# A fourth chunk by seven products in the gate/up groups of a two-layer decoder trunk, with merged combinations and h transposes in one bank

## The chip, the cores and the metric

The kernel runs on one core of a Trainium2 chip. TensorE (PE) multiplies matrices into PSUM, which has eight banks of 512 float32 columns; VectorE (DVE) and ScalarE (ACT) work element by element on SBUF and PSUM; SyncE (SP) issues most of the transfers. Each engine takes its instructions in the order in which they stand in its own list, and waits on semaphores for what other engines have to deliver. The metric is the device time of one execution, in microseconds (us).

## The reference

For 256 tokens of width 2048 two layers are computed: a token mixer (trailing means in layer 0, differential attention with eight heads in layer 1), then a dense SwiGLU block, each with an RMS norm in front and a residual addition behind.

```python
def swiglu(h, wg, wu, wd):
    return (jax.nn.silu(h @ wg) * (h @ wu)) @ wd
...
        h = h + mix
        h = h + swiglu(rmsnorm(h, norm_ffn[i]), w_gate[i], w_up[i], w_down[i])
    return rmsnorm(h, final_norm)
```

`w_gate` and `w_up` are 2048 x 5632, `w_down` is 5632 x 2048, all float32. The change is about `h @ wg` and `h @ wu`.

## The kernel before

**Precision.** Every large product is made from float32 numbers split in two: a rounded half `hi` (ScalarE, a cast) and the remainder `lo` (VectorE, a subtraction). One block product is three matmuls, hi by hi, hi by lo and lo by hi, each 128 x 128 by 128 x 512.

**Groups and chunks.** The 5632 columns of gate and up are done in 11 groups of 512 + 512 columns. A group runs over eight chunks of 256 weight rows (called p0 to p7 here), one 1 MB load each (`load`, three buffers `raw`). A chunk is a 2 x 2 by 2 x 2 block product: two halves of the tokens, two halves of the rows, gate and up. A *plain* chunk makes the eight block products, 24 matmuls. A chunk *by sevens* (`SEVEN`: p2, p4 and p6; in group 0 of layer 0 p6 alone) uses Winograd's scheme of seven products, 21 matmuls. For it VectorE makes four sums of weight blocks (`sums`, L121, L123, L124), ScalarE rounds them (`thi`, L130) and VectorE makes their remainder (`tlo`, L131); the weight halves `whi` (L115) and `wlo` (L116) then need only three of the four blocks. There is one buffer each for `tsum`, `thi` and `tlo`, and three for each of `whi` and `wlo`. The token sums are made once, where the operand is transposed (`pair`).

**Banks.** The products of all chunks of a group add up in the eight banks, named M1, M6, M7, P5, P3, P4, M2 and X (0 to 7); plain chunks use M2, P3, P4 and X. At the end of a group `combined` makes gate and up from them: two copies on ScalarE and eight additions on VectorE, of 512 columns each (L201 to L211). Then come silu (L463, ScalarE), the product with up (L464, VectorE), and for the two new pairs of h tiles four 128 x 128 transposes each (L250, PE), written to a bank from `aux`, which takes banks 0 to 3 in turn; ScalarE and VectorE read them into the operand of the down product (L254, L255, or L263 to L268 where the down product takes the pair by sevens).

**Order.** Groups come in chunks of 4, 4 and 3; after each such set there are two groups of the down product (`w_down`), with residual additions at their end (L487). The program is written in this order, and a scheduler of the framework, which has its own estimates, fixes the order in each engine's list. Loads, halves and sums of the next group's first chunks stand there ahead of or between the combinations of the group before.

## Time and profile before

| | |
|---|---|
| median of three runs | 1845.46 us (1845.2 to 1845.46) |
| profiled execution, its own time | 1846.21 us |
| its span from first to last instruction | 1844.4 us |
| granted TensorE clock, mean | 0.997 |
| PE / DVE / ACT busy | 1829.2 / 1604.2 / 1038.0 us |
| transfers | 356.80 MB, 193 GB/s |

A row of the profile that groups instructions has the line, the engine, the operation, out<-in by the program's names, the shapes and the count; behind the bar the busy time in us and the mean of one in ns; behind the second bar the engine's idle time before them and what ended it. A row of the timeline has the start and the duration in us; in brackets stands the idle time before it and who ended it. A row of a table of stretches has, for each engine, busy us and the count, then the granted clock, the share of the transfer engines and GB/s.

### The profile page before, as it was taken

The numbers are of one execution on the slowest core, as the hardware profiler recorded it, in microseconds if no ns is written. First come the engines' busy times: TensorE is split into PE (matmuls) and PEld (weight loads), VectorE is DVE, ScalarE is ACT, GpSimd is POOL, SyncE is SP. The second block draws the span as 40 slices with busy tenths as digits, with TensorE's granted clock in tenths as the row PEclk, the third lists the DMA queues.
The fourth block names the chain that finished last, engine by engine and source line by source line (L and its number), as shares of the span: only waits on it lengthen the run. The fifth ranks groups of instructions, "written<-read, shape, count | busy, mean of one in ns | idle before, by whom it ended". The sixth has DMA issues, their size and how long they took to land.

```text
span 1844.4 us, 20901 instructions
## 1 busy us (share of the span) xinstructions
PE 1829.2 (99%) x8210; PEld 1495.6 (81%) x8210; DVE 1604.2 (87%) x1662; ACT 1038.0 (56%) x1006; POOL 0.7 (0%) x6
## 2 busy tenths in 40 slices
PE   9999999999999999999999999999999999999998
PEld 6788888888888888888888888788888888888886
DVE  6889998898989899988888678998989899998986
ACT  6555555555554556665566655555555555545553
POOL 0000000000000000000000000000000000000000
PEclk9999999999999999999999999999999999999999
DMA  7555555655555555555454454555555555565552
GB/s 273 183 201 187 193 210 194 210 196 194 203 198 204 202 186 183 208 180 171 173 177 164 160 188 176 205 203 187 204 205 204 188 201 183 206 227 204 206 186 111
DMA packets 50642, 356.80 MB, mean 193 GB/s; under 512 B 6000, under 2 KB 6128, under 8 KB 8048
## 3 DMA queue, kind: packets, MB, share of 16 engines
q1 hardware_dynamic: 49824, 353.85, 54.4%
q10 hardware_dynamic: 720, 1.62, 0.2%
q8 instruction: 64, 1.05, 0.2%
q14 instruction: 34, 0.28, 0.0%
HBM read 353.36 MB, written 2.10 MB: 193 GB/s over the span
## 4 chain that ended last, share of the span: by engine, by line
PE 95%; DVE 2%; ACT 1%; issue 1%; DMA 1%; SPq 0%; DVEq 0%; ACTq 0%
PE b L180 90%; PE b L250 2%; PE b L342 1%; DVE wlo L116 1%; PE b L554 1%; PE b L345 1%; PE b L584 0%; DMA w<-pool_w 0%; DMA raw<-w_gu 0%; DVE tlo L131 0%; ACT whi L115 0%; DVE tsum L121 0%; PE b L600 0%; PE b L598 0%; PE b L599 0%
## 5 line engine op out<-in xcount | busy, mean ns | idle before, releaser
L115 ACT CAST whi<-raw 128x1536 fp32r<-128x1536 f32 (+1 forms) x330 | 585.2, 1774 | 585.4 <-PE b L180 499.6
L180 PE MATMUL b<-whi,xp 128*128 128x512 f32 x2824 | 908.8, 392 | 1.2 <-DVE c L203 1.0
L116 DVE TENSOR_TENSOR wlo<-raw,whi 128x1536 fp32r<-128x1536 f32 (+1 forms) x330 | 697.3, 2113 | 193.1 <-ACT whi L115 192.9
L180 PEld LDWEIGHTS b<-whi,xp 128*128 128x128 f32 x2824 | 528.3, 188 | 110.1 <-DVE c L203 1.5
L180 PE MATMUL b<-wlo,xp 128*128 128x512 f32 x1412 | 551.8, 391 | 1.6 <-DVE wlo L116 1.6
L180 PE MATMUL b<-whi,h 128*128 128x512 f32 x1108 | 354.5, 390 | 0.0
L180 PEld LDWEIGHTS b<-wlo,xp 128*128 128x128 f32 x1412 | 265.3, 188 | 55.5 <-DVE wlo L116 1.9
L131 DVE TENSOR_TENSOR tlo<-tsum,thi 128x2048 fp32r<-128x2048 f32 x108 | 246.7, 2285 | 3.9 <-ACT thi L130 3.9
L180 PEld LDWEIGHTS b<-whi,h 128*128 128x128 f32 x1108 | 207.5, 188 | 43.1
L180 PE MATMUL b<-wlo,h 128*128 128x512 f32 x554 | 215.8, 389 | 0.0
L130 ACT CAST thi<-tsum 128x2048 fp32r<-128x2048 f32 x108 | 206.3, 1910 | 13.7 <-DVE tsum L124 13.6
L180 PE MATMUL b<-thi,xp 128*128 128x512 f32 x608 | 211.8, 390 | 0.0
L121 DVE TENSOR_TENSOR tsum<-raw 128x1024 f32<-128x1024 f32 x108 | 131.8, 1220 | 2.3 <-DMA raw<-w_v 0.6
L180 PEld LDWEIGHTS b<-thi,xp 128*128 128x128 f32 x608 | 113.9, 188 | 24.0 <-ACT thi L130 0.9
L180 PEld LDWEIGHTS b<-wlo,h 128*128 128x128 f32 x554 | 104.0, 188 | 21.3
L180 PE MATMUL b<-tlo,xp 128*128 128x512 f32 x304 | 119.5, 393 | 0.0
L180 PE MATMUL b<-thi,h 128*128 128x512 f32 x240 | 83.7, 389 | 0.0
L124 DVE TENSOR_TENSOR tsum<-tsum,raw 128x512 f32<-128x512 f32 x108 | 74.3, 688 | 2.3
L123 DVE TENSOR_TENSOR tsum<-tsum,raw 128x512 f32<-128x512 f32 x108 | 73.9, 684 | 0.6
L180 PE MATMUL b<-whi,oT 128*128 128x512 f32 x236 | 74.4, 392 | 0.0
L180 PEld LDWEIGHTS b<-tlo,xp 128*128 128x128 f32 x304 | 57.0, 188 | 16.1 <-DVE tlo L131 4.4
L180 PEld LDWEIGHTS b<-thi,h 128*128 128x128 f32 x240 | 45.1, 188 | 9.2
(147 smaller groups left out, 1192.5 us busy)
## 6 DMA issues: line engine op xcount, KB each, us to landing
raw<-w_gu SPq DMA_DIRECT2D x176, 1024.0 KB, 4.9
raw<-w_down SPq DMA_DIRECT2D x88, 1024.0 KB, 4.8
raw<-w_qk SPq DMA_DIRECT2D x32, 1024.0 KB, 4.9
raw<-w_v SPq DMA_DIRECT2D x16, 1024.0 KB, 4.8
raw<-w_o SPq DMA_DIRECT2D x16, 1024.0 KB, 4.8
raw<-pool_w SPq DMA_DIRECT2D x2, 1024.0 KB, 13.8
x_tok<-x_n SPq DMA_DIRECT2D x2, 768.0 KB, 9.0
w<-pool_w SPq DMA_DIRECT2D x2, 512.0 KB, 6.6
```

Source lines behind the costliest of these rows:

```text
L115: nc.scalar.copy(hi[:, lo_block:], raw[:, lo_block:])
L116: nc.vector.tensor_tensor(lo[:, lo_block:], raw[:, lo_block:], f32(hi[:, lo_block:]), ALU.subtract)
L121: nc.vector.tensor_tensor(t[:, T1:T3 + 1], raw[:, B11:B22 + 1], raw[:, B12:B12 + 1].broadcast_to([P, 2, 512]), ALU.add)
L123: nc.vector.tensor_tensor(t[:, T2], t[:, T1], raw[:, B22], ALU.add)
L124: nc.vector.tensor_tensor(t[:, T4], t[:, T2], raw[:, B21], ALU.add)
L130: nc.scalar.copy(hi, t)
L131: nc.vector.tensor_tensor(lo, t, f32(hi), ALU.subtract)
L180: nc.tensor.matmul(ps[b], x, y[:, block], start=first, stop=(left[b] == 0))
L250: nc.tensor.transpose(ps[:, i, 1 - t if seven else t], src(i, t), ident)
L342: nc.tensor.matmul(yp[g][t], a[:, rows], w[:, at], start=(at == 0), stop=(at == 3))
L345: nc.tensor.matmul(yp[g][t], u, v[:, at], start=(at == 0 and j == 0), stop=(at == 3 and j == 2))
L554: nc.tensor.matmul(sc[:, :nk], qk[:, 0, c, qb * P:(qb + 1) * P], qk[:, 1, c, :nk], start=True, stop=True)
```

## The change

`SEVEN` becomes (0, 2, 4, 6): p0 is done by sevens too, in groups 1 to 10 of both layers (group 0 of layer 0 keeps p6 alone, group 0 of layer 1 keeps p2, p4 and p6). In a chunk by sevens the three products of raw weight blocks come first (P3 only late in a group's first chunk), and the products of sums follow. P3 and P4 become one tile of two banks, b45, and `combined` works on both at once: two subtractions become one of 1024 columns (L211), two additions one (L212). The transposes of h go to bank X (7) instead of the banks 0 to 3. To make room in SBUF for p0's larger operand, constants live shorter (`ones`, `dist_sb`, whose load moves to the attention's start), `part` uses other small tiles, and four of the heads' outputs use the operand's buffers.

```diff
-SEVEN = (2, 4, 6)
+SEVEN = (0, 2, 4, 6)
...
+    def two_banks():
+        both = psum.tile([P, 2, 512], F32, name="b45", tag="b45")
+        return [both[:, i] for i in range(2)], both
...
             if seven:
-                plan.append([(M1, [(A11, 0, B11)]), (M2, [(A12, 0, B21)]), (M6, [(S2, 1, T2)]), (M7, [(S3, 1, T3)]),
-                             (P5, [(S1, 1, T1)]), (P3, [(S4, 0, B22)]), (P4, [(A22, 1, T4)])])
+                raw = [(M1, [(A11, 0, B11)]), (M2, [(A12, 0, B21)]), (P3, [(S4, 0, B22)])]
+                summed = [(P5, [(S1, 1, T1)]), (M7, [(S3, 1, T3)]), (M6, [(S2, 1, T2)]), (P4, [(A22, 1, T4)])]
+                late = 3 if plan else 2
+                plan.append(raw[:late] + summed[:3] + raw[late:] + summed[3:])
...
-            first = b not in ps
-            if first:
+            first = b not in opened
+            opened.add(b)
+            if first and b in (P3, P4) and b not in ps:
+                (ps[P3], ps[P4]), ps["both"] = two_banks()
+            elif first and b not in ps:
                 ps[b] = bank(b)
...
-        m1, u2, u3, p5 = (pool.tile([P, 512], F32, name=f"c{i}") for i in ("11", "12", "21", "22"))
+        c = pool.tile([P, 4, 512], F32, name="c")
+        m1, u2, u3, p5 = (c[:, i] for i in range(4))
...
-        nc.vector.tensor_tensor(u2, p5, u2, ALU.subtract)
-        nc.vector.tensor_tensor(p5, p5, u3, ALU.subtract)
-        nc.vector.tensor_tensor(u2, ps[P3], u2, ALU.add)
-        nc.vector.tensor_tensor(u3, ps[P4], u3, ALU.add)
+        nc.vector.tensor_tensor(c[:, 1:4:2], c[:, 3:4].broadcast_to([P, 2, 512]), c[:, 1:3], ALU.subtract)
+        nc.vector.tensor_tensor(c[:, 1:3], ps["both"], c[:, 1:3], ALU.add)
...
-    def pair(dst, src, gains, seven):
+    def pair(dst, src, gains, seven, at=None):
 
-        ps = aux((P, 2, 2, P))
+        ps = aux((P, 2, 2, P)) if at is None else bank(at, (P, 2, 2, P))
...
-                    by_seven = SEVEN[-1:] if g == 0 and layer == 0 else SEVEN
+                    by_seven = SEVEN if g else SEVEN[1:] if layer else SEVEN[-1:]
...
-                        pair(ht, lambda k, t: cs[t][1][:, (2 * i + k) * P:(2 * i + k + 1) * P], None, at in SEVEN_DOWN)
+                        pair(ht, lambda k, t: cs[t][1][:, (2 * i + k) * P:(2 * i + k + 1) * P], None, at in SEVEN_DOWN, X)
...
+        dist_sb = hq.tile([P, 2 * P], F32, name="dist_sb")
+        nc.sync.dma_start(out=dist_sb, in_=dist)
```

In the changed kernel the sums are L120, L122 and L123, whi L114, wlo L115, thi L129, tlo L130, the matmuls L184, the combinations L206 to L214, silu L469, the product with up L470, the h transposes L253, their reads L257, L258 and L266 to L271, the residual additions L493. There are 20 groups that begin with p0 by sevens: 16 follow a gate/up group, four a down group. The lists differ at the transitions, in three ways.

**Place one, VectorE between the third and the fourth group of layer 0** (c is the third group's gate and up; with a prime for the next group, wlo_1407 and tsum_1398 belong to p0', wlo_1441 to p1', raw_1468 and wlo_1475 to p2'). Before:

```order
L116 TENSOR_TENSOR wlo_1441<-raw_1438,whi_1440 128x2048
L207 TENSOR_TENSOR c22_1367<-c22_1367,c21_1366 128x512
L208 TENSOR_TENSOR c12_1365<-b4_1114,c12_1365 128x512
L209 TENSOR_TENSOR c21_1366<-b5_1121,c21_1366 128x512
L211 TENSOR_TENSOR c22_1367<-b7_1128,c22_1367 128x512
L464 SCALAR_TENSOR_TENSOR c12_1365<-c12_1365,r_tok_496,c11_1364 128x512
L464 SCALAR_TENSOR_TENSOR c22_1367<-c22_1367,r_tok_496,c21_1366 128x512
L123 TENSOR_TENSOR tsum_1470<-tsum_1470,raw_1468 128x512
L116 TENSOR_TENSOR wlo_1475<-raw_1468,whi_1474 128x1536
```

Of the changed kernel:

```order
L209 TENSOR_TENSOR c_1361<-b2_1120,c_1361 128x512
L123 TENSOR_TENSOR tsum_1398<-tsum_1398,raw_1396 128x512
L211 TENSOR_TENSOR c_1361<-c_1361 128x2x512
L115 TENSOR_TENSOR wlo_1475<-raw_1468,whi_1474 128x1536
L212 TENSOR_TENSOR c_1361<-b45_1128,c_1361 128x1024
L214 TENSOR_TENSOR c_1361<-b7_1159,c_1361 128x512
L470 SCALAR_TENSOR_TENSOR c_1361<-c_1361,r_tok_496 128x512 x2
L130 TENSOR_TENSOR tlo_1407<-tsum_1398,thi_1406 128x2048
```

The remainder of p2' (wlo_1475) has moved from behind the combinations to ahead of the last two, and a new tlo, of p0', stands behind them. Eight of the 16 transitions between gate/up groups have this order.

**Place two, PE at the same transition** (xp_76, xp_78 and xp_79 are the operands of p0', p2' and p3' in the changed kernel, xp_83 that of p0' before; the transposes are those on ident). Before:

```order
L180 MATMUL b5_1424<-whi_1406,xp_83 128x512
L250 MATMUL b2_1383<-ident_75,c12_1365 128x128
L250 MATMUL b3_1397<-ident_75,c12_1365 128x128
L180 MATMUL b5_1424<-whi_1406,xp_83 128x512
L180 MATMUL b5_1424<-wlo_1407,xp_83 128x512
L250 MATMUL b2_1383<-ident_75,c22_1367 128x128
```

Of the changed kernel, from the 15th matmul behind the group's last one on:

```order
L184 MATMUL b6_1414<-wlo_1475,xp_78 128x512
L184 MATMUL b6_1414<-whi_1474,xp_78 128x512
L184 MATMUL b45_1430<-whi_1402,xp_76 128x512
L184 MATMUL b45_1430<-wlo_1403,xp_76 128x512
L184 MATMUL b45_1430<-whi_1402,xp_76 128x512
L184 MATMUL b45_1430<-thi_1406,xp_76 128x512
L253 MATMUL b7_1375<-ident_74,c_1361 128x128 x4
L184 MATMUL b6_1414<-whi_1505,xp_79 128x512
L253 MATMUL b7_1389<-ident_74,c_1361 128x128 x4
L184 MATMUL b3_1418<-tlo_1407,xp_76 128x512
```

Between a group's last matmul and the first that reads tlo of p0' there stand 23 matmuls now (11 on thi of p0' or behind it, up to the transposes), and all eight transposes, of which the second four wait until bank 7 has been read.

**Place three: ScalarE between the sixth and the seventh group of layer 0** (c_2811 is the sixth group; whi_2924 belongs to p2', thi_2856 to p0', whi_2955 to p3', e and h are reads of the h transposes; before, whi_2939 belongs to p2' and whi_2974 to p3'), **and VectorE from a down group to gate/up.** ScalarE before:

```order
L463 ACTIVATE c11_2829<-c11_2829,r_tok_496 128x512
L115 CAST whi_2939<-raw_2933 128x1536
L463 ACTIVATE c21_2831<-c21_2831,r_tok_496 128x512
L263 ACTIVATE e_2853<-b0_2848 128x256
L263 ACTIVATE e_2853<-b0_2848 128x2x128
L254 CAST h_2861<-b1_2862 128x2x256
L115 CAST whi_2974<-raw_2972 128x2048
```

Of the changed kernel:

```order
L469 ACTIVATE c_2811<-c_2811,r_tok_496 128x512
L114 CAST whi_2924<-raw_2918 128x1536
L129 CAST thi_2856<-tsum_2848 128x2048
L469 ACTIVATE c_2811<-c_2811,r_tok_496 128x512
L114 CAST whi_2955<-raw_2953 128x2048
L266 ACTIVATE e_2830<-b7_2825 128x256
```

A thi has come in behind whi of p2' and ahead of the second silu. On VectorE there the order is L212, L214, the first L470, tlo of p0', the second L470, wlo of p1'; seven transitions are like this. VectorE from a down group to gate/up before (wlo_2306 belongs to p1', tsum_2335 to p2'):

```order
L487 TENSOR_TENSOR x_tok_82<-c22_2254,x_tok_82 128x512
L116 TENSOR_TENSOR wlo_2306<-raw_2303,whi_2305 128x2048
L123 TENSOR_TENSOR tsum_2335<-tsum_2335,raw_2333 128x512
L116 TENSOR_TENSOR wlo_2340<-raw_2333,whi_2339 128x1536
L124 TENSOR_TENSOR tsum_2335<-tsum_2335,raw_2333 128x512
```

Of the changed kernel (wlo_2292 belongs to p1', tsum_2250 and tlo_2259 to p0'):

```order
L212 TENSOR_TENSOR c_2235<-b45_1986,c_2235 128x1024
L214 TENSOR_TENSOR c_2235<-b7_1999,c_2235 128x512
L493 TENSOR_TENSOR x_tok_75<-c_2235,x_tok_75 128x512 x3
L123 TENSOR_TENSOR tsum_2250<-tsum_2250,raw_2248 128x512
L115 TENSOR_TENSOR wlo_2292<-raw_2289,whi_2291 128x2048
L130 TENSOR_TENSOR tlo_2259<-tsum_2250,thi_2258 128x2048
```

The last sum of p0' now stands behind the residual additions, and its tlo behind wlo of p1'; ahead of the first matmul on thi of p0' PE has 12 matmuls.

More of the change, by code (lines that the diff above doesn't have):

```diff
@@ L84, in trunk_kernel @@
     gain_sb = const.tile([P, 6, NK], F32, name="gain_sb")
-    dist_sb = const.tile([P, 2 * P], F32, name="dist_sb")
     ident = const.tile([P, P], F32, name="ident")
-    ones = const.tile([P, P], F32, name="ones")
-    nc.vector.memset(ones, 1.0)
-    make_identity(nc, ident)
     x_tok = resid.tile([P, 2, D], F32, name="x_tok")
@@ L152, in group @@
                 left[b] = left.get(b, 0) + 3 * len(parts)
-        ps = {}
+        ps, opened = {}, set()
         def prepared(seven, src):
@@ L280, in trunk_kernel @@
     with tc.tile_pool(name="start", bufs=1, reuse_waits="tile") as st:
+        ones = st.tile([P, P], F32, name="ones")
+        nc.vector.memset(ones, 1.0)
         warm = tmp.tile([P, 8], F32, name="warm", bufs=1)
+        make_identity(nc, ident)
         nc.scalar.activation(warm[:, 0:1], ones[:, 0:1], AF.Sqrt)
@@ L334, in product @@
             if some[0] == 0:
-                yp[g] = [bank(4 + 2 * (g % 2) + t) for t in range(2)]
+                yp[g] = [bank(6 + t) for t in range(2)] if g % 2 else two_banks()[0]
                 if g >= PLAIN:
@@ L413, in trunk_kernel @@
     turn["of"] = 4
-    nc.sync.dma_start(out=dist_sb, in_=dist)
     def finish(cs, ys, final_sb, ss):
         for t in range(2):
-            part = tmp.tile([P, 64], F32, name="part", bufs=2)
+            part = tmp.tile([P, 8], F32, name="warm", bufs=1) if t == 0 else \
+                tmp.tile([P, 2, 4], F32, name="ss").rearrange("p a b -> p (a b)")
             nc.vector.tensor_reduce(part[:, 0:1], ss[:, t, 0:2], AX.X, ALU.add)
@@ L515, in trunk_kernel @@
         nc.vector.tensor_scalar(qs_col, r_col, QK_SCALE, None, ALU.mult)
+        ones = hq.tile([P, P], F32, name="ones")
+        nc.vector.memset(ones, 1.0)
         nc.vector.tensor_tensor(lp, lam_sb[:, 0:2], lam_sb[:, 2:4], ALU.mult)
@@ L608, in trunk_kernel @@
                     nc.scalar.activation(on[:, t, :], op[:, t, :], AF.Copy, scale=ro[:, t:t + 1])
-                oT[h] = op_.tile(pair_shape(h in SEVEN_O), F32R, name=f"oT{h}")
+                if h < 4:
+                    oT[h] = op_.tile(pair_shape(h in SEVEN_O), F32R, name=f"oT{h}")
+                else:
+                    oT[h] = resid.tile(pair_shape(h in SEVEN_O), F32R, name="xp", tag=f"xp{h}")
                 pair(oT[h], lambda i, t: on[:, t, i * P:(i + 1) * P], [gs[:, i:i + 1] for i in range(2)], h in SEVEN_O)
```

## The prediction

> **What bounds the kernel now.** I read the page first: busy shares, then the chain that ended last.
>
> ```profile
> PE 1829.2 (99%) x8210; PEld 1495.6 (81%) x8210; DVE 1604.2 (87%) x1662; ACT 1038.0 (56%) x1006; POOL 0.7 (0%) x6
> ...
> PE 95%; DVE 2%; ACT 1%; issue 1%; DMA 1%; SPq 0%; DVEq 0%; ACTq 0%
> PE b L180 90%; PE b L250 2%; PE b L342 1%; DVE wlo L116 1%; PE b L554 1%; PE b L345 1%; PE b L584 0%; DMA w<-pool_w 0%; DMA raw<-w_gu 0%; DVE tlo L131 0%; ACT whi L115 0%; DVE tsum L121 0%; PE b L600 0%; PE b L598 0%; PE b L599 0%
> ```
>
> TensorE sets the end: 90% of the chain are the matmuls of L180. VectorE's 87% is a mean, so I looked at single stages: two gate/up groups (eight chunks and eight h transposes each) and one down group without transposes.
>
> ```profile
> core 0: us, PE busy (x) PEld busy (x) DVE busy (x) ACT busy (x) POOL busy (x), PEclk, DMA share, GB/s
> 340.00:382.43 42.43, 42.43 (x193) 35.09 (x192) 37.66 (x33) 23.06 (x18) 0.00 (x0) 1.00 0.57 198
> 425.15:467.88 42.73, 42.73 (x193) 35.01 (x192) 38.87 (x37) 24.18 (x20) 0.00 (x0) 1.00 0.56 197
> 510.62:552.10 41.48, 41.48 (x185) 34.35 (x184) 37.56 (x34) 20.64 (x14) 0.00 (x0) 1.00 0.57 203
> ```
>
> The down group issues 3 x 21 + 5 x 24 = 183 matmuls in 41.48 us (two of the 185 counted overlap the edges): 0.2267 us each. The same 183 with eight transposes take 42.73, so the transposes cost 1.25. In that gate/up group VectorE has only 42.73 - 38.87 = 3.86 us left.
>
> **The change part by part.** Removed: 20 chunks (chunk 0 of groups 1 to 10, both layers) go from 24 matmuls to 21: 60 x 0.2267 = 13.6 us of TensorE. Added on VectorE and ScalarE, by these rows:
>
> ```profile
> L116 DVE TENSOR_TENSOR wlo<-raw,whi 128x2048 fp32r<-128x2048 f32 x222 | 508.1, 2289 | 178.8 <-ACT whi L115 178.7
> L131 DVE TENSOR_TENSOR tlo<-tsum,thi 128x2048 fp32r<-128x2048 f32 x108 | 246.7, 2285 | 3.9 <-ACT thi L130 3.9
> L130 ACT CAST thi<-tsum 128x2048 fp32r<-128x2048 f32 x108 | 206.3, 1910 | 13.7 <-DVE tsum L124 13.6
> L116 DVE TENSOR_TENSOR wlo<-raw,whi 128x1536 fp32r<-128x1536 f32 x108 | 189.2, 1752 | 14.3 <-ACT whi L115 14.2
> L115 ACT CAST whi<-raw 128x1536 fp32r<-128x1536 f32 x108 | 160.4, 1485 | 210.0 <-PE b L180 157.1 <-DVE c L209 33.7 <-issue 16.8
> L487 DVE TENSOR_TENSOR x_tok<-c,x_tok 128x512 f32<-128x512 f32 x44 | 28.3, 683 | 0.0
> L254 ACT CAST h<-b 128x512 fp32r<-128x512 f32 x28 | 15.9, 592 | 12.5 <-PE b L250 12.5
> ```
>
> What VectorE holds up is less than a duration, since the next one starts before the last has ended. The timeline of a transition between groups shows the steps, and what ScalarE waits for there:
>
> ```profile
> 425.75 1.22 DVE L121 TENSOR_TENSOR tsum<-raw 128x1024 f32<-128x1024 f32 x1
> 426.88 0.68 DVE L204 TENSOR_TENSOR c<-b,c 128x512 f32<-128x512 f32 x1
> 427.48 0.68 DVE L203 TENSOR_TENSOR c<-b,c 128x512 f32<-128x512 f32 x1
> ...
> 428.68 2.28 DVE L116 TENSOR_TENSOR wlo<-raw,whi 128x2048 fp32r<-128x2048 f32 x1
> 430.88 0.68 DVE L207 TENSOR_TENSOR c<-c,c 128x512 f32<-128x512 f32 x1
> ...
> 433.28 1.40 DVE L464 SCALAR_TENSOR_TENSOR c<-c,r_tok,c 128x512 f32<-128x512 f32 x2
> 434.60 0.68 DVE L123 TENSOR_TENSOR tsum<-tsum,raw 128x512 f32<-128x512 f32 x1
> 435.20 1.75 DVE L116 TENSOR_TENSOR wlo<-raw,whi 128x1536 fp32r<-128x1536 f32 x1
> 436.87 0.41 DVE L264 TENSOR_TENSOR e<-e 128x256 f32<-128x256 f32 x1
> ```
> ```profile
> 431.24 1.48 ACT L115 CAST whi<-raw 128x1536 fp32r<-128x1536 f32 x1 [2.32 <-PE b L180]
> 432.80 0.72 ACT L463 ACTIVATE c<-c,r_tok 128x512 f32<-128x512 f32 x1
> 435.63 0.66 ACT L263 ACTIVATE e<-b 128x256 f32<-128x256 f32 x2 [2.11 <-PE b L250]
> ```
>
> From start to start: 2.20 for 2048 columns, 1.67 for 1536, 1.13 for 1024, 0.60 for 512, 0.66 for L464. One more seven costs VectorE 1.13 + 2 x 0.60 + 2.20 - (2.20 - 1.67) = 4.0 us. No row shows the merged combinations (L211, L212); they lie between L121's 1.13, the same size, and two single steps, 1.20. I take 1.13, which saves 4 x 0.60 - 2 x 1.13 = 0.14 a group. So VectorE needs 38.87 + 3.86 = 42.73 in such a group, TensorE 42.73 - 0.68 = 42.05: **VectorE has no spare time left**, and whatever it does late TensorE feels.
>
> Late it will be at the transitions. Write p0 to p7 for a group's chunks, p0' for the next group's, and T for the moment at which TensorE could issue the matmul behind the group's last. The weight halves have three buffers, so whi of p2' takes p7's and cannot start before T + 0.2: a matmul lasts 0.39 by the row below, 0.16 beyond the next issue, and the reader's start is rounded up.
>
> ```profile
> L180 PE MATMUL b<-whi,xp 128*128 128x512 f32 x2824 | 908.8, 392 | 1.2 <-DVE c L203 1.0
> ```
>
> The row at 431.24 is that wait: 2.32 us, and harmless, because p0' and p1' were plain chunks, prepared, with 48 matmuls (10.9 us) for TensorE. Now p0' is a seven. Its raw products are 9 matmuls; the other 12 need thi and tlo.
>
> *Transitions of the first kind* (8 of 16; front part, places one and two). ScalarE: whi of p2' ends at T + 1.7. VectorE has wlo of p2' ahead of L212: 1.7 + 1.67 = 3.4; L212 to 4.5, L214 to 5.1, two L470 to 6.4, tlo of p0' to 8.7. ScalarE goes on with silu (0.72) and thi of p0' (1.91), to T + 4.25; from there TensorE has 11 matmuls to 6.75 and four h transposes (half of 1.25) to 7.4. The second four want the same bank, which ScalarE reads behind whi of p3'; that cast waits for P3 of p0' (T + 6.7) and ends at 8.65, the two reads (0.66) at 9.3. The transposes end at T + 10.0, and only then come the matmuls on tlo. Done by then: 23 x 0.2267 + 1.25 = 6.5 us. **Lost: 3.5 us.** Where both h pairs are plain (4 of the 8) the bank is free after a cast (0.59, from 8.65) and a subtraction (0.68), transposes end at 10.5, and 28 matmuls and the eight transposes are done, 7.6: lost 2.9.
>
> *Second kind* (7; place three, ScalarE). thi of p0' stands behind whi of p2': T + 1.7 + 1.9 = 3.6. Then tlo to 5.9, the second L470 to 6.5, wlo of p1' to 8.8. Ahead of wlo of p1' TensorE has 24 matmuls and the transposes, 6.7: lost 2.1. The next sums (of p2') end on VectorE about T + 15.3, their cast behind whi of p4' at 17.4, while 57 matmuls and 1.25 are 14.2: 3.2 lost in all.
>
> *From a down group to gate/up* (4; place three, VectorE). L212 can end at T + 0.8, L214 at 1.4, three residual adds (L487's step 0.60) at 3.2, the last sum at 3.8, thi at 5.8. TensorE has 12 matmuls, 2.7: lost 3.1. Nothing is lost there now.
>
> The first transition of layer 0 has p0' fully prepared: 0. From gate/up to down, p0' stays plain: 0. **Sum:** 4 x 3.5 + 4 x 2.9 + 7 x 3.2 + 4 x 3.1 = 60.4, less 13.6: +46.8. At the low end only the first waits count (2.2 from tlo's T + 8.7 against 6.5; 2.1; 3.1): 8 x 2.2 + 7 x 2.1 + 12.4 - 13.6 = +31. At the high end VectorE, without spare time, adds 1 us to each of the 16: +63.
>
> At no cost I take: raw products first (they only cover more); the merged sums outside gate/up, where VectorE is not late; the loads, equal in number, with dist's moved among them on SP's queue; and p0's operand laid out for sevens, 1.2 us more of VectorE twice, which if not covered is +2.4.
>
> **The clock.** Stalls of 3 us may also lower it. Two stretches of the profile's clock grid, each with what followed:
>
> ```profile
> 4.80:8.21 3.41, 1.80 (x12) 1.20 (x11) 1.36 (x3) 0.72 (x2) 0.00 (x0) 1.00 0.96 340
> 8.21:11.62 3.41, 3.41 (x7) 1.39 (x6) 0.48 (x1) 0.67 (x1) 0.00 (x0) 0.50 1.03 429
> 52.58:56.00 3.42, 1.77 (x10) 1.31 (x9) 2.73 (x2) 3.11 (x5) 0.00 (x0) 1.00 0.24 34
> 56.00:59.41 3.41, 3.13 (x16) 2.36 (x15) 3.41 (x5) 1.32 (x3) 0.00 (x0) 1.00 0.68 279
> ```
>
> TensorE was busy 1.80 of 3.41 us, and the next 3.41 ran at 0.50; busy 1.77, and they ran at 1.00. The margin lies near there, and the single 3.1 us gap behind a down group would pass it; a stretch at half clock costs 3.41 / 2 = 1.7 us. The Trainium skill, "TensorE: Matmul & The Clock Gate", section "What's actually happening", says that the clock is halved after at least one idle window of about 3.4 us. By that rule none of my gaps halves it, and the sum stays; the first of the rows above does not bear it out, since that window was half busy.
>
> **The rivals.** (1) *TensorE stays the bound*: what is late hides behind products that the new order finds. 1846.2 - 13.6, less 0.75 for the median: 1832. For it: 99% busy now, and waits of VectorE and ScalarE hidden everywhere. Against it: rows of fixed order and duration behind one fixed event, T. (2) *VectorE becomes the bound and keeps pace*: 16 groups with a seven among their h at 42.73 as now, the four others at 41.75 instead of 42.43: -2.7, 1843, no change. Against it: it must never wait, and it waits 1.5 us for whi of p2' at half the transitions. (3) *The half clock*: the four gaps behind down groups and the seven of the second kind, each up to 1.7: +19, 1911. It decides from the point at which a gap fills about half a window. (4) *Loads late as well*: chunk p5's buffer comes free only with p2's last sum, and landing takes 4.9:
>
> ```profile
> raw<-w_gu SPq DMA_DIRECT2D x176, 1024.0 KB, 4.9
> ```
>
> With that VectorE is a further 2 us late in 16 groups: +79 in all, 1924.
>
> **How the numbers follow.** The sum is made on the profiled execution, 1846.2, which is 0.75 above the median: 1846.2 + 46.8 - 0.75 = 1892. Chances: my forecast 0.66, (1) 0.09, (2) 0.06, (3) 0.12, (4) 0.07. The forecast's own range is 1872 to 1910. To 1864 at the low end for transitions that lose less, to 1926 at the high end for (3) and (4). A measurement of this kernel tells about 0.2% (3.7 us) from no change: faster 0.09, same 0.06, slower 0.85.
>
> **What would show it.** In the changed profile: 60 fewer matmuls; PE's share under 97%; idle time of PE and PEld before L184 and L253 on tlo, thi and wlo, 2 to 4 us at a transition; gate/up groups of 44 to 45.5 us followed by gate/up, under 42.3 where down follows; ScalarE's whi on 1536 columns still released by PE at T. Wrong would be: transitions without idle TensorE (1), VectorE without any idle time in a group (2), a clock under 0.99 (3), or whi waiting for raw<-w_gu (4).

## The result and the profile after

The changed kernel takes 1933.85 us (median of 4 runs, 1933.13 to 1934.39) where the kernel before took 1845.33 beside it: a ratio of 1.048, 95% interval 1.0461 to 1.0498. It is slower, as forecast, but by 88.5 us instead of 46.8, and 8 us above the range's upper end.

The page of the changed kernel: the busy shares, and the chain that ended last, by engine and by line.

```profile
PE 1858.0 (96%) x8150; PEld 1480.3 (77%) x8150; DVE 1682.2 (87%) x1665; ACT 1055.3 (55%) x1028; POOL 0.7 (0%) x6
...
PE 75%; DVE 12%; ACT 6%; issue 4%; DMA 3%; SPq 0%; ACTq 0%; DVEq 0%
```

60 matmuls fewer, as planned, and TensorE's part of the chain falls from 95% to 75%: VectorE (12%, before 2%) and ScalarE (6%, before 1%) now stand in it. VectorE's busy share is the same 87%, but of a span 88 us longer. The waits show what TensorE misses (engine, line, releaser; then us in total, times, longest):

```profile
ACT whi L114 <- PE b L184: 369.9, 150, 6.3
ACT thi L129 <- DVE tsum L123: 161.5, 47, 5.4
DVE wlo L115 <- ACT whi L114: 111.7, 90, 4.2
DVE tlo L130 <- ACT thi L129: 89.9, 56, 2.1
ACT whi L114 <- DMA raw<-w_gu: 79.6, 55, 3.2
PEld b L184 <- ACT thi L129: 49.9, 69, 3.5
...
PEld b L184 <- DVE tlo L130: 25.9, 49, 2.0
PE b L184 <- ACT thi L129: 25.0, 23, 3.0
```

VectorE now waits 89.9 us for thi, where the row of L131 before had 3.9. The loads are late too: 79.6 us, where that wait came to 4.4 before.

A table of stretches, from each group's end to the next group's end (T to T): the first gate/up group behind a down group, the other three of the set, then the two down groups.

```profile
314.26:360.99 46.73, 43.63 (x183) 34.73 (x182) 40.86 (x32) 21.87 (x14) 0.00 (x0) 0.96 0.51 183
360.99:406.69 45.70, 43.21 (x189) 33.83 (x188) 40.91 (x36) 24.81 (x19) 0.00 (x0) 1.00 0.49 181
406.69:452.90 46.21, 43.80 (x189) 33.99 (x188) 42.67 (x38) 25.32 (x20) 0.00 (x0) 1.00 0.52 183
452.90:499.37 46.47, 43.76 (x189) 33.79 (x187) 42.99 (x36) 24.93 (x19) 0.00 (x0) 1.00 0.55 196
499.37:543.54 44.17, 43.02 (x193) 35.12 (x192) 40.98 (x38) 23.75 (x19) 0.00 (x0) 1.00 0.58 212
543.54:585.56 42.02, 42.02 (x185) 34.13 (x183) 36.48 (x32) 19.98 (x13) 0.00 (x0) 1.00 0.46 162
```

42.43 and 42.73 became 45.7 to 46.7. In the group of 46.21 VectorE is busy 42.67, almost exactly the need that the prediction worked out (42.73), and still 3.54 idle. The last of the four, which a down group follows, was expected under 42.3 and took 46.47. The first down group became longer too (42.75 before, 44.17), and the second (41.48, 42.02).

**Where the 88 us are.** From the first matmul behind every group's end in both traces:

| step, T to T | number | forecast | measured | of it half clock |
|---|---|---|---|---|
| gate/up to gate/up | 15 | +37.8 | +56.0 | 1.7 |
| down to gate/up | 4 | +9.7 | +21.8 | 8.5 |
| gate/up to down | 6 | 0 | +7.0 | 0 |
| down to down | 4 | 0 | +2.2 | 0 |
| first transition of layer 0 | 1 | -0.7 | -0.6 | 0 |
| all other work | | 0 | +1.7 | 0 |
| sum | | +46.8 | +88.1 | 10.2 |

88.1 is the difference of the two spans, 1932.5 - 1844.4. The forecasts are those of the prediction with the 0.68 us of the three saved matmuls taken off in each of 20 groups. The half clock of the last column is six stretches of 3.41 us at a granted clock of 0.50, 1.7 us lost in each; such stretches at the very start or end of the program, which the kernel before has too, are not counted. Of "all other work" 1.7 us lie in the last down group (43.60 against 41.94).

### The profile page after: what moved, and what is told of

Its sections match the earlier page's. It is cut to its first block, busy times and chain, and to the rows that moved or that the text cites. A ratio compares the mean times of both kernels' runs of the same rounds, so it can differ in the third digit from the quotient of the medians.

```text
span 1932.5 us, 20736 instructions
## 1 busy us (share of the span) xinstructions
PE 1858.0 (96%) x8150; PEld 1480.3 (77%) x8150; DVE 1682.2 (87%) x1665; ACT 1055.3 (55%) x1028; POOL 0.7 (0%) x6
## 4 chain that ended last, share of the span: by engine, by line
PE 75%; DVE 12%; ACT 6%; issue 4%; DMA 3%; SPq 0%; ACTq 0%; DVEq 0%
PE b L184 71%; DVE wlo L115 3%; ACT whi L114 3%; ACT thi L129 2%; DMA raw<-w_gu 2%; DVE tlo L130 2%; PE b L253 1%; DVE c L211 1%; DVE c L212 1%; DVE tsum L120 1%; DVE c L208 1%; DVE c L209 1%; PE b L564 1%; DVE c L207 1%; DMA x_tok<-x_n 1%
## 5 line engine op out<-in xcount | busy, mean ns | idle before, releaser
L184 PE MATMUL b<-whi,xp 128*128 128x512 f32 x2732 | 877.4, 394 | 7.7 <-ACT whi L114 4.5
L114 ACT CAST whi<-raw 128x1536 fp32r<-128x1536 f32 (+1 forms) x330 | 574.3, 1746 | 478.8 <-PE b L184 369.9
L115 DVE TENSOR_TENSOR wlo<-raw,whi 128x1536 fp32r<-128x1536 f32 (+1 forms) x330 | 685.7, 2080 | 112.6 <-ACT whi L114 111.7
L184 PEld LDWEIGHTS b<-whi,xp 128*128 128x128 f32 x2732 | 514.4, 189 | 124.5 <-ACT whi L114 10.3
L184 PE MATMUL b<-wlo,xp 128*128 128x512 f32 x1366 | 538.1, 394 | 0.3 <-DVE wlo L115 0.2
L130 DVE TENSOR_TENSOR tlo<-tsum,thi 128x2048 fp32r<-128x2048 f32 x128 | 293.1, 2290 | 91.2 <-ACT thi L129 89.9
L184 PE MATMUL b<-whi,h 128*128 128x512 f32 x1108 | 353.1, 392 | 5.7 <-DVE c L212 5.5
L129 ACT CAST thi<-tsum 128x2048 fp32r<-128x2048 f32 x128 | 244.1, 1907 | 194.6 <-DVE tsum L123 161.5
L184 PEld LDWEIGHTS b<-wlo,xp 128*128 128x128 f32 x1366 | 258.2, 189 | 54.0 <-DVE wlo L115 1.5
L184 PE MATMUL b<-thi,xp 128*128 128x512 f32 x784 | 272.4, 406 | 25.3 <-ACT thi L129 25.0
L184 PEld LDWEIGHTS b<-whi,h 128*128 128x128 f32 x1108 | 207.8, 188 | 53.3 <-DVE c L212 8.0
L184 PE MATMUL b<-wlo,h 128*128 128x512 f32 x554 | 216.1, 390 | 0.0
L184 PEld LDWEIGHTS b<-thi,xp 128*128 128x128 f32 x784 | 143.9, 191 | 75.1 <-ACT thi L129 49.9
L184 PE MATMUL b<-tlo,xp 128*128 128x512 f32 x392 | 156.8, 400 | 12.7 <-DVE tlo L130 12.7
L120 DVE TENSOR_TENSOR tsum<-raw 128x1024 f32<-128x1024 f32 x128 | 156.1, 1220 | 2.7 <-DMA raw<-w_v 1.4
L184 PEld LDWEIGHTS b<-wlo,h 128*128 128x128 f32 x554 | 104.1, 188 | 20.6
L184 PEld LDWEIGHTS b<-tlo,xp 128*128 128x128 f32 x392 | 74.3, 190 | 37.4 <-DVE tlo L130 22.8
L123 DVE TENSOR_TENSOR tsum<-tsum,raw 128x512 f32<-128x512 f32 x128 | 88.1, 688 | 2.2
L122 DVE TENSOR_TENSOR tsum<-tsum,raw 128x512 f32<-128x512 f32 x128 | 87.7, 685 | 0.4
L184 PE MATMUL b<-thi,h 128*128 128x512 f32 x240 | 78.9, 390 | 0.0
L469 ACT ACTIVATE c<-c,r_tok 128x512 f32<-128x512 f32 x44 | 31.8, 722 | 43.0 <-DVE c L212 23.0
L184 PEld LDWEIGHTS b<-thi,h 128*128 128x128 f32 x240 | 45.1, 188 | 9.1
```

The costliest lines, as they stand in the source:

```text
L114: nc.scalar.copy(hi[:, lo_block:], raw[:, lo_block:])
L115: nc.vector.tensor_tensor(lo[:, lo_block:], raw[:, lo_block:], f32(hi[:, lo_block:]), ALU.subtract)
L120: nc.vector.tensor_tensor(t[:, T1:T3 + 1], raw[:, B11:B22 + 1], raw[:, B12:B12 + 1].broadcast_to([P, 2, 512]), ALU.add)
L122: nc.vector.tensor_tensor(t[:, T2], t[:, T1], raw[:, B22], ALU.add)
L123: nc.vector.tensor_tensor(t[:, T4], t[:, T2], raw[:, B21], ALU.add)
L129: nc.scalar.copy(hi, t)
```

## Experiments

Three theories stood behind the experiments. F: the loss is a fixed chain behind a group's end, and it hurts because p0', the first chunk, is a seven. C: VectorE has no time for a fourth seven, wherever it stands. O: the merged combinations and the bank of the transposes cost by themselves. All times below stand beside runs of the kernel before on the same chip, 1845.7 to 1845.9.

**Three sevens again, the rest of the change kept.**

```diff
-SEVEN = (0, 2, 4, 6)
+SEVEN = (2, 4, 6)
```

> Only the fourth seven is undone (chunks p2, p4, p6 again); the merged combinations, raw products first and the h transposes in bank X stay. Theory F (chunk p0' by sevens leaves TensorE too little prepared work behind a group's end): back to before, 1840 to 1850 us. Theory C (VectorE has no spare time for four sevens wherever they stand): the same, 1840 to 1850. Theory O (the merged combinations and the one bank for h cost by themselves): stays above 1880 us.

Measured: 1857.52 us, ratio 1.0062 (1.0047 to 1.0077). None of the forecasts holds (1840 to 1850, or above 1880). The fourth seven costs 76 us, everything else 12. That 12 was no part of the forecast, which had put the merge at -0.14 a group and the order and the bank at nothing.

**The four sevens on the odd chunks.**

```diff
-SEVEN = (0, 2, 4, 6)
-SEVEN_QKV = (4, 6)
-SEVEN_O = (6,)
+SEVEN = (1, 3, 5, 7)
+SEVEN_QKV = (5, 7)
+SEVEN_O = (7,)
```

> Four sevens as in the change, but in chunks p1, p3, p5, p7 (the attention's two products by sevens move to p5 and p7, and its output product's to p7, for the operand's buffers), so that a group starts with a plain chunk. Theory F: the waits behind a group's end on thi and tlo of the first chunk go, gate/up groups fall from about 46 to 42 to 43 us, 1835 to 1860 us in all. Theory C: VectorE does the same work, groups stay at 45 us and more, above 1900 us.

Measured: 1998.13 us, ratio 1.082 (1.0802 to 1.0838). F's forecast fails: with p0 plain again the loss grows. C's, above 1900, holds, but it gives no reason for so much, and two more things are in it. The half clock takes 41 us here (24 stretches of 3.41 us at a clock of 0.50, against six and 10.2 us in the changed kernel). And with p7 by sevens the sums' products come last in a group; the waits of TensorE are now for a combination that has to read a bank:

```profile
PE b L184 <- DVE c L208: 52.0, 27, 3.1
```

L208 reads bank M2, which the next group's plain p0 needs first. The kernel moves the pressure to another place, so it speaks against F and tells little about C.

**One remainder left out in mid-group.** tlo of p4 in the gate/up groups is not made, and its matmuls read thi in its place.

```diff
+        if no_lo:
+            nc.scalar.copy(hi, t)
+            return hi, hi
         nc.scalar.copy(hi, t)
         nc.vector.tensor_tensor(lo, t, f32(hi), ALU.subtract)
```

> The change, with the remainder of the weight sums left out in the middle chunk p4 of the gate/up groups: no VectorE subtraction there (2.2 us a group less), and the matmuls on it read the rounded sums instead; TensorE's work stays. Theory F: the transitions lose as before, at most the waits later in a group get shorter: 1910 to 1934 us. Theory C: all of VectorE's saving comes back, 2.2 x 20 = 44 us: 1890 us or less.

Measured: 1865.66 us, ratio 1.0106 (1.0086 to 1.0126), in C's range and not in F's: 68 us less for 46 us of VectorE work (21 remainders of 2.20), at a place that is not in the transition's chain at all. The other 22 us are not explained by the work left out. The framework fixes the order of the lists anew for every edit, and counted from the two traces at least 206 of VectorE's 1644 instructions stand at another place than in the changed kernel. The loss at the transition is gone. VectorE's timeline in this kernel; the third gate/up group of layer 0 ends at T = 177.45:

```profile
172.21 0.68 DVE L123 TENSOR_TENSOR tsum<-tsum,raw 128x512 f32<-128x512 f32 x1
...
175.31 2.29 DVE L133 TENSOR_TENSOR tlo<-tsum,thi 128x2048 fp32r<-128x2048 f32 x1
177.51 1.22 DVE L215 TENSOR_TENSOR c<-b,c 128x1024 f32<-128x1024 f32 x1
```

The same in the changed kernel, where that group ends at T = 179.98, and ScalarE beside it:

```profile
179.96 0.68 DVE L208 TENSOR_TENSOR c<-b,c 128x512 f32<-128x512 f32 x1
180.56 0.68 DVE L209 TENSOR_TENSOR c<-b,c 128x512 f32<-128x512 f32 x1
181.16 0.68 DVE L123 TENSOR_TENSOR tsum<-tsum,raw 128x512 f32<-128x512 f32 x1
181.76 1.22 DVE L211 TENSOR_TENSOR c<-c 128x1024 f32<-128x1024 f32 x1
182.89 1.75 DVE L115 TENSOR_TENSOR wlo<-raw,whi 128x1536 fp32r<-128x1536 f32 x1
184.56 1.22 DVE L212 TENSOR_TENSOR c<-b,c 128x1024 f32<-128x1024 f32 x1
...
187.62 2.28 DVE L130 TENSOR_TENSOR tlo<-tsum,thi 128x2048 fp32r<-128x2048 f32 x1
```
```profile
180.22 1.48 ACT L114 CAST whi<-raw 128x1536 fp32r<-128x1536 f32 x1 [3.22 <-PE b L184]
...
182.23 1.88 ACT L129 CAST thi<-tsum 128x2048 fp32r<-128x2048 f32 x1
```

With the remainder left out, the last of p0's sums (L123) stands 5.2 us before T and p0's tlo is done by T + 0.1; in the changed kernel the sum starts at T + 1.2 and tlo runs from T + 7.6 to T + 9.9. So the order that the prediction walked through is there (whi at T + 0.2, tlo behind L212, its matmuls from about T + 10), but it isn't fixed behind T. It is what a VectorE that arrives late looks like; one that has gained 2.2 us in every group has the sums and their remainder done before T.

**VectorE's work without the fourth seven.** A test of C in which p0 stays plain: three sevens, and a remainder written a second time, which changes nothing in the result: in p4 alone (2.2 us a group), then in p2 and p4 (4.4, where the fourth seven adds 4.0).

```diff
-        nc.vector.tensor_tensor(lo, t, f32(hi), ALU.subtract)
+        for _ in range(times):
+            nc.vector.tensor_tensor(lo, t, f32(hi), ALU.subtract)
```

> Three sevens (p0 plain, as in the run with three sevens, 1857.5 us) and the remainder of the sums (tlo, 2.29 us, pitch 2.20) of chunk p4 written a second time in every gate/up group: 2.2 us of VectorE work more, about half of what the fourth seven adds (4.0), and no fourth seven. Theory C (VectorE's time in a group, its forced waits included, sets the period): the groups of the changed kernel show 42.5 us busy and 3.2 to 4.7 us of waits in 46.2; a group of three sevens has about 39 busy, so 41.2 and about 3 of waits make 44.2 where TensorE needs 42.5; over 16 groups up to 27 us more, 1870 to 1885. Theory F (only a first chunk by sevens leaves TensorE too little prepared work behind a group's end): under 1862, since the order of work at a group's end is that of three sevens.

> Three sevens (p0 plain) and the remainder of the sums of chunks p2 and p4 written twice: 4.4 us of VectorE work more in a gate/up group, a little more than the fourth seven adds, and no fourth seven; 60 more matmuls than the changed kernel. Theory C: 39 + 4.4 busy and about 3 of waits make 46.4 against 42.5: 16 groups of 3.9 us, 62 us over 1857.5, so 1905 to 1935 with what the clock takes. Theory F: under 1867.

Measured: 1876.61 us (1.0166; 1.0146 to 1.0187) and 1925.3 us (1.043; 1.0409 to 1.0451). Against three sevens that is +19 for the first 2.2 us a group and +49 more for the second. F, which expected under 1862 and 1867, falls: p0 is plain, and the time is lost all the same. The curve bends: the first half still finds some room, the second none. The added work is not the only difference: here, too, the lists have a new order, and against three sevens at least 111 and 198 of VectorE's 1581 instructions stand at another place. So these runs show what the work costs together with the order that it brings, not the work alone.

The bend can be read from one cycle of layer 0, four gate/up and two down groups. Tables of stretches of before, of three sevens, of the two kernels above, of the changed kernel, and of the one with a remainder left out (span; PE, PEld, DVE, ACT, POOL busy; clock; transfers):

```profile
304.37:557.95 253.58, 253.58 (x1132) 208.82 (x1130) 229.39 (x202) 136.86 (x100) 0.00 (x0) 1.00 0.56 199
```
```profile
305.44:561.04 255.60, 254.61 (x1132) 208.04 (x1130) 228.63 (x190) 135.29 (x100) 0.00 (x0) 1.00 0.55 198
```
```profile
308.75:567.65 258.90, 255.86 (x1131) 208.05 (x1130) 236.84 (x194) 134.87 (x100) 0.00 (x0) 1.00 0.54 195
```
```profile
314.88:582.78 267.90, 258.52 (x1132) 207.13 (x1131) 245.25 (x198) 135.20 (x100) 0.00 (x0) 1.00 0.53 189
```
```profile
314.26:585.56 271.30, 259.44 (x1120) 205.59 (x1118) 244.90 (x206) 140.67 (x104) 0.00 (x0) 0.99 0.52 186
```
```profile
304.55:561.82 257.27, 252.79 (x1119) 205.56 (x1118) 235.90 (x202) 141.50 (x104) 0.00 (x0) 1.00 0.54 196
```

| | cycle | VectorE busy | VectorE idle |
|---|---|---|---|
| before | 253.58 | 229.39 | 24.2 |
| three sevens | 255.60 | 228.63 | 27.0 |
| remainder left out in p4 | 257.27 | 235.90 | 21.4 |
| remainder twice in p4 | 258.90 | 236.84 | 22.1 |
| remainder twice in p2 and p4 | 267.90 | 245.25 | 22.7 |
| changed kernel | 271.30 | 244.90 | 26.4 |

In these six kernels VectorE's idle time stays between 21 and 27 us in six groups, 3.6 to 4.5 in each, with 6 to 16 us more work as with none. (Where something else delays it, it is higher: 32.5 us with the odd chunks.) From the fourth row to the fifth it gets 8.4 us more to do, and the cycle becomes 9.0 us longer. With that idle time TensorE's 253.6 us a cycle leave VectorE about 232; the fourth seven asks for 245. What the idle time consists of, in the same cycle of the kernel before and of the changed kernel:

```profile
DVE wlo L116 <- ACT whi L115: 23.3, 19, 1.6
```
```profile
DVE tlo L130 <- ACT thi L129: 17.4, 11, 2.1
DVE wlo L115 <- ACT whi L114: 7.8, 7, 2.5
```

It is the wait for ScalarE's cast of the chunk whose remainder stands next in VectorE's order. Before, too, it was nearly all of VectorE's idle time (23.3 of 24.2). But what stands behind the cast is not the same. VectorE between a chunk's last sum and its remainder (tlo), before and in the changed kernel:

```profile
457.43 0.69 DVE L124 TENSOR_TENSOR tsum<-tsum,raw 128x512 f32<-128x512 f32 x1
459.59 2.29 DVE L116 TENSOR_TENSOR wlo<-raw,whi 128x2048 fp32r<-128x2048 f32 x1 [1.46 <-ACT whi L115]
461.80 2.28 DVE L131 TENSOR_TENSOR tlo<-tsum,thi 128x2048 fp32r<-128x2048 f32 x1
```
```profile
442.25 0.69 DVE L123 TENSOR_TENSOR tsum<-tsum,raw 128x512 f32<-128x512 f32 x1
445.00 2.29 DVE L130 TENSOR_TENSOR tlo<-tsum,thi 128x2048 fp32r<-128x2048 f32 x1 [2.05 <-ACT thi L129]
```

Before, a wlo stands in between, and thi is rounded behind it. All 19 waits of the cycle are for whi, and in 15 of them ScalarE had itself waited until TensorE released a weight buffer. In the changed kernel tlo often stands right behind the last sum: VectorE ends the sum, ScalarE rounds it, and VectorE waits, 2.05 us in 8 of the 18 waits, 16.4 of the 25.2 us. So it is idle time of about the same length, but of another kind. No run puts other work between that sum and its remainder, so how much of the loss is the order of the list stays open.

**The sums of p0 and p4 on GpSimd**, to take 4.7 us a group off VectorE again.

```diff
-            t = sums(pool, raw) if seven else None
+            t = sums(pool, raw, nc.gpsimd if seven == "pool" else None) if seven else None
```

> The changed kernel with the column sums (tsum, three instructions) of the gate/up chunks p0 and p4 on GpSimd instead of VectorE: 2 x 2.33 us of pitch less on VectorE in a group, which puts its need below that with three sevens. Theory C: TensorE bounds the groups again, 1857.5 - 13.6 = 1844 us and up to 25 us for the groups behind a down group, so 1844 to 1870. Theory F: tsum of p0 comes later still, so over 1915. A third (P): GpSimd's sums take VectorE's time away or are several times slower than VectorE's 0.6 us for 512 columns, no trace shows them yet: 1880 to 1930.

Measured: 2009.48 us, ratio 1.0884 (1.0866 to 1.0902), so P, and beyond its range. Of the 75.6 us over the changed kernel 49.5 are half clock (35 stretches of 3.41 us, 59.7 us, against 10.2). GpSimd's rows, and VectorE's wlo of 2048 columns in this kernel:

```profile
L121 POOL TENSOR_TENSOR tsum<-raw 128x1024 f32<-128x1024 f32 x41 | 113.4, 2766 | 1579.4 <-DVE tlo L131 1498.1 <-DVE e L270 81.3
L123 POOL TENSOR_TENSOR tsum<-tsum,raw 128x512 f32<-128x512 f32 x41 | 105.3, 2568 | 3.2
L124 POOL TENSOR_TENSOR tsum<-tsum,raw 128x512 f32<-128x512 f32 x41 | 101.6, 2479 | 3.2
```
```profile
L115 DVE TENSOR_TENSOR wlo<-raw,whi 128x2048 fp32r<-128x2048 f32 x202 | 505.6, 2503 | 106.1 <-ACT whi L114 105.4
```

A chunk's sums take 7.8 us there instead of VectorE's 2.3, and they start only when tlo has been made from the last sums (one buffer of `tsum`). And VectorE does not become free: 123 instructions fewer, but 1684.3 us busy against 1682.2, since some of the others take longer (wlo 2503 ns in the mean instead of 2287). The Trainium skill, "Trainium Architecture — The Big Picture", section "What this means for kernel authors", says that VectorE and GpSimd share an SBUF port pair under an exclusive lock; the longer wlo fits it, though no run here tells a lock from another kind of contention. This run does not test C, because it adds a delay of its own.

**Which of the other parts costs the 12 us.** Three sevens with one part undone each: the products' old order; a bank each for P3 and P4 with four combinations of 512 columns; the h transposes in banks 0 to 3.

```diff
-                plan.append(raw[:late] + summed[:3] + raw[late:] + summed[3:])
+                plan.append([(M1, [(A11, 0, B11)]), (M2, [(A12, 0, B21)]), (M6, [(S2, 1, T2)]), (M7, [(S3, 1, T3)]),
+                             (P5, [(S1, 1, T1)]), (P3, [(S4, 0, B22)]), (P4, [(A22, 1, T4)])])
```
```diff
-        nc.vector.tensor_tensor(c[:, 1:3], ps["both"], c[:, 1:3], ALU.add)
+        nc.vector.tensor_tensor(u2, ps[P3], u2, ALU.add)
+        nc.vector.tensor_tensor(u3, ps[P4], u3, ALU.add)
```
```diff
-                        pair(ht, ..., None, at in SEVEN_DOWN, X)
+                        pair(ht, ..., None, at in SEVEN_DOWN)
```

> Three sevens, and the products inside a chunk by sevens in the order of the kernel before (M1, M2, M6, M7, P5, P3, P4); the combinations over two banks and the h transposes in bank 7 stay. Three sevens alone took 1857.5 against 1845.7 before; its trace shows the 14 down groups 0.54 us longer each (42.02 against 41.48, two waits for tlo inside a group, 7.5 us in all) and the groups behind a down group 1.6 us longer. If the new order of products is what costs: 1845 to 1850. If the merged combinations or the bank cost it: 1855 to 1860.

> Three sevens with a bank each for P3 and P4 and four combinations of 512 columns instead of two of 1024; the new order of products and the h transposes in bank 7 stay. If the merge is what costs the 12 us of three sevens (both banks come free only when one long instruction has read both): 1845 to 1850. If the order of the products or the bank of the transposes costs it: 1855 to 1860.

> Three sevens with the h transposes in the next of banks 0 to 3 as before, the rest as in the changed kernel. Bank 7 is read last by the combinations and taken by the next group's second chunk, which may hold the transposes or the chunk up: if this is what costs, 1845 to 1852. If the order or the merge costs it: 1855 to 1862.

Measured: 1866.38 us (1.0112; 1.0097 to 1.0127), 1849.8 us (1.0023; 1.0013 to 1.0032) and 1857.16 us (1.0059; 1.0042 to 1.0076). The bank of the transposes costs nothing that shows. The merge costs 7.7 us, although it saves VectorE a little work. The old order in all groups together with the merge makes things worse by 9, the other way round than expected. With single banks 4 us are left. By the traces each second down group of the first two sets of a layer is longer (42.04 against 41.48), and so are the two gate/up groups behind it (42.02 against 41.48, 43.27 against 42.43). That is 1.9 us in each of four places; most of the other gate/up groups and the first down groups are 0.2 shorter. So the new order was kept in the gate/up groups alone:

```diff
+                if early:
+                    plan.append(raw[:late] + summed[:3] + raw[late:] + summed[3:])
+                else:
+                    plan.append(raw[:2] + summed[2:0:-1] + summed[:1] + raw[2:] + summed[3:])
```

> Three sevens, a bank each for P3 and P4, four combinations, and the new order of products in the gate/up groups alone; down, q/k, v and output groups keep the order of the kernel before. Three sevens with single banks took 1849.8 with the down groups at 42.04 against 41.48 before: 14 x 0.55 = 7.7 us to be had back if the order of products costs them that, so 1842 to 1844, a little faster than before (1845.7). If the down groups are longer for another reason: 1848 to 1851.

Measured: 1845.39 us, ratio 0.9999 (0.999 to 1.0008). The 4 us are back, so the order of products in the other groups was their cause (second down groups at 41.48 again, the gate/up groups behind them at 41.7 to 42.0 and 42.5). The 1842 to 1844 expected were not reached: that forecast counted 0.55 us for 14 down groups, where four show it, and the first down groups now take 42.81, with single banks 42.53. It is the best version with any part of the change, and no faster than the kernel before: what the new order gains in some gate/up groups (42.5 against 42.73) is no more than a measurement can tell.

The merge was also undone in the changed kernel itself, with all four sevens:

> The change without the merged combinations: P3 and P4 are two banks again, with two subtractions and two additions of 512 columns on VectorE. Theory F: the same within 8 us of 1934. Theory C: 0.14 us more VectorE a group, 1934 to 1940. Theory O (an addition that waits for both banks is what costs): below 1915 us.

Measured: 1926.97 us, ratio 1.0438 (1.0417 to 1.0459): 7 us less than the changed kernel, about as with three sevens. O has the sign, but its forecast, under 1915, fails: the merge costs 7 us of 88. The time lies within F's 8 us of 1934 and under C's 1934, but neither theory has a term for the merge, so this run doesn't decide between them. By which wait the merge costs is not settled for the groups that combine; with three sevens the second gate/up group of a set takes 44.06 us merged and 43.27 single. One part is seen at the end of the program: the last down group, which is read bank by bank and combines nothing, takes 43.63 and 41.94 us. There the two banks only share a tile, and the waits of L431 (L430) for TensorE grow from 5.2 us to 7.9.

**Are late loads a cause of their own?** Four sevens with three and with four load buffers. To make room, both do p2 and p6 of the down groups plain and keep fewer buffers in the first stage.

```diff
-    wraw = ctx.enter_context(tc.tile_pool(name="wraw", bufs=3))
+    wraw = ctx.enter_context(tc.tile_pool(name="wraw", bufs=4))
```

> The changed kernel with the down groups' chunks p2 and p6 plain instead of by sevens and fewer buffers in the first stage: it is the control of the run with four load buffers. Two chunks more with 24 matmuls more each per... in all about 14 down groups of 6 more matmuls (3 a chunk for the 24 against 21 of a block of products): +19 us at 0.2267, less what VectorE's spare time in the down groups gives back behind them (up to 16): 1930 to 1955.

> The same with four load buffers instead of three, so that a chunk's load starts a chunk earlier. If late loads (79.6 us of ScalarE waiting for raw in the changed kernel) are a cause of their own: 20 to 60 us less than with three buffers. If VectorE's time is the cause and the loads are late only since everything before them is: within 10 us of it.

Measured: 1907.05 us (1.0332; 1.0313 to 1.0351) and 1896.61 us (1.0275; 1.0257 to 1.0294): the fourth buffer gives 10 us, at the edge between the two expectations. About half is the half clock (10.3 us of it with three buffers, 5.1 with four). With three buffers ScalarE's wait for loads is 32.9 us in this kernel, with four it is gone. So late loads are a small cause beside VectorE's time, not the main one; in the changed kernel, where the wait is 79.6, they were not tested. The control is a surprise: it came out 23 us under its forecast's lower end. Its down groups have six matmuls more each, and yet it is 27 us faster than the changed kernel: its plain chunks leave VectorE less to do, 1598.3 us busy instead of 1682.2. VectorE gets ahead in the down groups and spends the lead in the first gate/up groups behind them. From the table of stretches with four buffers, the second and the third gate/up group of a set:

```profile
358.08:399.88 41.80, 41.80 (x190) 34.52 (x188) 37.62 (x34) 23.09 (x19) 0.00 (x0) 1.00 0.44 155
399.88:447.18 47.30, 45.08 (x191) 35.50 (x189) 41.73 (x33) 23.13 (x18) 0.00 (x0) 0.96 0.52 186
```

The second runs at TensorE's pace with four sevens, 41.80; the third takes 5.5 longer. A mean over the cycle hides that: with three buffers the cycle takes 266.58 us with VectorE busy for only 227.30, less than before the change. VectorE's spare time lies in the down groups and the work in the gate/up groups; that the three buffers of halves carry little from one to the other is a reading, not tested.

## Why the prediction came out as it did

- **Direction, and the likeliest case: right.** VectorE could not carry a fourth seven, and TensorE waits behind it on tlo and thi as named (for wlo hardly, 1.7 us in all). 60 matmuls went and PE's share is 96%. The size is off: 88.5 us instead of 46.8, gate/up groups of 45.7 to 46.7 instead of 44 to 45.5.
- **The step that failed: "In that gate/up group VectorE has only 42.73 - 38.87 = 3.86 us left".** Those 3.86 us were taken for spare time that the new work may fill. VectorE's need was set at 42.73, work alone, against TensorE's 42.05, and what went beyond that was priced only behind T. The work came out as forecast, 42.67 in the group of 46.21, but VectorE is idle for 3.54 us of it all the same, most of it between a last sum and its remainder, while ScalarE rounds the sum. That 42.67 and 3.54 make 46.21 would be so in any group; the evidence is that the idle time stays at 3.6 to 4.5 us a group in all six kernels of the table. The high end of the range had 1 us a group for this.
- **The walk behind T: right in its steps, wrong as a frame.** whi starts at T + 0.2 as forecast, thi ends at 4.1 (4.25); VectorE's part is 1.2 us late, L212 from 4.6 (3.4) and tlo to 9.9 (8.7), since L208, L209, the last sum (L123) and L211 kept it until T + 2.9. TensorE's matmuls on tlo, forecast for T + 10.0 behind the transposes, came at T + 9.98, in part by luck: tlo, expected 1.3 us ahead of the last transpose, ended with it. But it treats each loss as the price of one transition, caught up by its end. The group walked lost 7.4 us of TensorE's time, only half of it in the first 11 us. In the runs with a remainder left out and written twice the price goes with VectorE's work, whether p0 is a seven or not. In the table: 18.2 us too little for gate/up to gate/up.
- **"From gate/up to down, p0' stays plain: 0": wrong, +7.0.** VectorE's lateness reaches L212, and the first down products wait for its bank. Part of it is the merge's: with four sevens and single banks the group of 44.17 takes 43.1.

```profile
L184 PE MATMUL b<-whi,h 128*128 128x512 f32 x1108 | 353.1, 392 | 5.7 <-DVE c L212 5.5
```

- **"At no cost I take": wrong by 12 with three sevens.** The merge costs 7 to 8 us, in which a saving of 0.14 a group was expected; the new order outside gate/up costs 4 us, although raw products first "only cover more". In the changed kernel the +2.2 from down to down are this, 0.55 in each; with three sevens the group behind shows as much again (42.02 against 41.48).
- **Rival (3), the half clock, came in part**: 10.2 us of the 19. It was counted as an alternative; it came on top. The four gaps behind down groups were 3.0 us each, forecast 3.1.
- **Rival (4), late loads, came as a small part**: whi does wait for its loads, 79.6 us in all. Four buffers instead of three give 10 us, in a kernel in which the wait was 32.9. Rival (1) and (2) did not come.
- **The range** treated (3) and (4) as other cases. That its own upper end, 1910, with the clock's 10 and the 12 of the other parts gives 1932 is found after the fact and explains nothing: the upper end is not what the transitions cost.

## What to carry to other kernels

Idle time of the second-busiest engine is spare only so far as it isn't a wait that every unit of work brings with it: before spending it, list what ended it, and what that in turn had waited for. Whether an engine has room is cheaply measured by writing one of its results twice: here 2.2 us a group cost 19 us in all, 4.4 cost 68, with the lists' order changed along with it. Compare the lists before an experiment's time is put down to its edit. An instruction merged to save time can cost more than it saves: here 7 us.

## What the runs showed of the hardware beside this

Gaps of the same length did not always halve the clock. Stretches of the changed kernel's clock grid around three of the four gaps behind down groups, and around one transition between gate/up groups (third column PE busy, the clock third from the end):

```profile
317.12:320.53 3.41, 0.37 (x3) 0.31 (x3) 3.41 (x4) 1.90 (x1) 0.00 (x0) 1.00 0.41 103
320.53:323.94 3.41, 3.41 (x10) 2.65 (x9) 3.41 (x2) 0.80 (x1) 0.00 (x0) 0.50 1.02 408
...
586.77:590.18 3.41, 1.67 (x8) 1.05 (x6) 3.41 (x6) 1.16 (x2) 0.00 (x0) 1.00 0.00 0
590.18:593.59 3.41, 2.11 (x9) 1.75 (x10) 3.41 (x2) 1.25 (x1) 0.00 (x0) 1.00 0.85 305
...
637.97:641.38 3.41, 2.00 (x9) 1.26 (x10) 3.41 (x4) 1.97 (x2) 0.00 (x0) 1.00 0.00 0
641.38:644.79 3.41, 3.41 (x12) 2.84 (x11) 3.41 (x3) 0.59 (x1) 0.00 (x0) 0.50 0.00 0
...
1443.51:1446.93 3.42, 1.31 (x6) 0.75 (x4) 3.42 (x5) 1.18 (x2) 0.00 (x0) 1.00 0.14 17
1446.93:1450.34 3.41, 2.48 (x6) 2.00 (x7) 3.41 (x3) 0.87 (x1) 0.00 (x0) 0.50 0.87 344
```

The four gaps behind down groups are 3.04 us each. One that lies in one stretch (0.37 us busy) was followed by half clock. Divided between two stretches (1.67 and 2.11 busy) it left the clock alone at 590, but not at 1446.93, where 1.31 was left. And a stretch with 2.00 busy, its idle time in several short waits, was followed by half clock, while 1.67 was not. So busy time in a stretch alone does not decide it. The Trainium skill, "TensorE: Matmul & The Clock Gate", section "What's actually happening", says that the window is free-running and that one idle window throttles; the fixed grid of 3.41 us agrees, the idle window does not: the three stretches shown ahead of a half clock were all partly busy, 0.37, 1.31 and 2.00 us.

GpSimd's addition of 512 float32 columns took 2.5 us, VectorE's 0.69, and in the kernel in which GpSimd worked VectorE's wlo took up to 4.5 us, twice its median (shortest, median and longest in ns, of all forms):

```profile
L115 DVE TENSOR_TENSOR wlo<-raw,whi x330: 1741/2283/4497, 20.4 to 1983.0; 128x1536 fp32r<-128x1536 f32 x128, 128x2048 fp32r<-128x2048 f32 x37
```
